# Softmax over rows of 512: two loads queued when group 8 has been scaled, and a store directly behind them

## The chip, the cores and the metric

The kernel runs on one core of a Trainium2 chip. The metric is the device time of one execution in microseconds (us), the median of several runs. The engines that matter are VectorE (DVE), ScalarE (ACT), GpSimd (POOL) and SyncE (SP). SyncE computes nothing here: it waits on semaphores and issues the DMA transfers, all of them into one queue that is served by 16 DMA engines.

## The reference

```python
x = np.random.randn(16, 1024, 512).astype(np.float32)

def reference(x):
    x_max = np.max(x, axis=-1, keepdims=True)
    exp_x = np.exp(x - x_max)
    return (exp_x / np.sum(exp_x, axis=-1, keepdims=True)).astype(np.float32)
```

It is a softmax over the last axis: 16,384 rows of 512 numbers. The input is 33.55 MB and the output as much.

## The kernel before

The rows are dealt to the 128 partitions, so each partition has 128 rows. Eight rows of every partition are a group, and there are 16 groups. Two groups, 16 rows or 4 MB, are a block; every transfer moves one block, so there are 8 loads and 8 stores. In this document load n and store n are those of block n, which holds groups 2n and 2n+1.

The data stays in one buffer in SBUF, `held`, in which all is computed in place. It is a ring of 12 groups (`RING`), six blocks. Loads 0 to 5 therefore fill it, and load 6 goes to the place of block 0, load 7 to that of block 1, once stores 0 and 1 have landed.

For each group, VectorE takes the row maxima with the sign changed (`rowmax`, line 169). ScalarE takes the exponential of each row with that as its bias and sums it (line 213). VectorE takes the reciprocal of the sums (line 177). Then the group is multiplied by it (`scale`, line 183), on GpSimd for groups 0 to 11 and on VectorE for groups 12 to 15. The string `VECTOR` gives VectorE's order by hand: M for maxima, P for a reciprocal whose product GpSimd makes, V for one whose product VectorE makes. The end of a group's product raises the semaphore `scaled[g]`.

SyncE's order is written out in `ORDER`: loads 0 to 5 (`AHEAD` of them without a wait), stores 0 to 2, loads 6 and 7, stores 3 to 7. SyncE runs through this list strictly in order; a wait holds up everything behind it. The loop of lines 144 to 158 puts the waits in:

- Ahead of a load it waits for the store that frees the place (line 148).
- Ahead of a store it waits for `scaled` of the store's two groups, and for one more group where `AFTER` names one (line 153). Each group is waited for once, at the first place that asks for it (`done`).

`AFTER` is `{(0, 16): 4, (48, 64): 11, (80, 96): 12}`: store 0 also waits for group 4, store 3 for group 11 and store 5 for group 12. The helper `take` (line 114) is a wait on a semaphore that sets it back.

Of the kernel before, what the change touches and what calls it, by code (L numbers as in the profile page):

```python
# [14 lines left out]
GROUPS = 16  # L15
# [25 lines left out]

AFTER = {(0, 16): 4, (48, 64): 11, (80, 96): 12}

# [29 lines left out]
def kernel(  # L77
# [5 lines left out]
    nc = tc.nc  # L83
# [7 lines left out]
    def in_dram(rows, a, b):  # L91

        first, last = next(k for k in BLOCKS if k[0] <= a and b <= k[1])
        block = rows[first * P : last * P].rearrange("(p r) d -> p r d", p=P)
        return block[:, a - first : b - first, :]
# [9 lines left out]
    scaled = [nc.alloc_semaphore(f"scaled{g}") for g in range(GROUPS)]  # L105
# [6 lines left out]
    def take(engine, semaphore, n):  # L112

        engine.wait_ge(semaphore, n).then_inc(semaphore, -n)  # L114

    def rows(a, b):
        assert a // RING == (b - 1) // RING
        return held[:, a % RING : (b - 1) % RING + 1, :]

    def meets(k, a, b):  # L120
        return k[0] < b and a < k[1]

    def group(g):
        return g * GROUP, (g + 1) * GROUP
# [4 lines left out]
    def load(k):  # L129
        copy = nc.sync.dma_start(out=rows(*k), in_=in_dram(x_rows, *k))  # L130
        copy.then_inc(loaded[k], 16)
        return copy
# [9 lines left out]

    taken, done = set(), set()
    for what, k in ORDER[AHEAD:]:
        if what == "L":
            for s in stores:
                if meets(s, k[0] - RING, k[1] - RING) and s not in taken:
                    take(nc.sync, stored[s], 16)
                    taken.add(s)
            load(k)  # L150
        else:
            for g in range(GROUPS):
                if (meets(k, *group(g)) or AFTER.get(k) == g) and g not in done:
                    take(nc.sync, scaled[g], 1)
                    done.add(g)
            nc.sync.dma_start(out=in_dram(out_rows, *k), in_=rows(*k)).then_inc(
                stored[k], 16
            )
# [34 lines left out]
    for step in VECTOR.split():  # L193
        what, g = step[0], int(step[1:])
# [62 lines left out]
```

## Time and profile before

| what | value |
|---|---|
| median of 3 runs | 159.81 us (159.57 to 159.94) |
| profiled execution | 160.33 us, of which its span from first to last instruction 159.0 us |
| VectorE, ScalarE, GpSimd busy | 90.0, 92.0, 83.9 us |
| DMA | 2304 packets, 67.11 MB, 422 GB/s over the span |
| load, issue to landing | median 30.3 us of 8, 4096 KB each |
| store, issue to landing | median 21.6 us of 8, 4096 KB each |

A load or store is issued by SyncE and then stands in the queue; issue to landing holds the time in the queue too. SyncE's instructions are not counted as busy. A transfer's issue is called by line 130 if it is a load and by line 156 if it is a store. The profiled execution lies 0.52 us above the median of the runs, and 1.33 us of it lie outside the span.

### The profile page before, as it was taken

What the parts mean: (1) busy time and instruction counts of PE and PEld (TensorE: products, weight loads), DVE (VectorE), ACT (ScalarE), POOL (GpSimd) and SP (SyncE); (2) the same over time, 40 slices, a digit from 0 to 9 for tenths busy, and PEclk for the clock granted to TensorE, in tenths of its full rate; (3) what the DMA queues carried; (4) which work ended last, traced back from release to release, by engine and by line L of the source; (5) the groups of instructions that cost most, each with busy time, mean ns of one, the idle gap of its engine ahead of it and who ended that gap; (6) DMA issues with size and microseconds to landing.
All of it is one profiled execution on the core that took longest, in us unless ns stands there. A gap on an engine that the chain in (4) does not pass through costs nothing. (4 is left out here: it accounts for less than half of the span.)

```text
span 159.0 us, 720 instructions
## 1 busy us (share of the span) xinstructions
DVE 90.0 (57%) x36; ACT 92.0 (58%) x257; POOL 83.9 (53%) x16
## 2 busy tenths in 40 slices
DVE  0008959777977977887700000695999996920000
ACT  0300699999999999999993000049946749000000
POOL 0000009999999999999999999990000000000000
DMA  7999999999999999999999999999999999999994
GB/s 264 453 462 404 404 503 412 396 453 462 404 396 511 412 396 437 478 404 396 503 412 404 387 396 495 429 396 445 478 396 396 495 429 396 429 486 404 396 495 173
DMA packets 2304, 67.11 MB, mean 422 GB/s; under 512 B 256, under 2 KB 256, under 8 KB 256
## 3 DMA queue, kind: packets, MB, share of 16 engines
q1 hardware_dynamic: 2304, 67.11, 98.5%
HBM read 33.55 MB, written 33.55 MB: 422 GB/s over the span
## 5 line engine op out<-in xcount | busy, mean ns | idle before, releaser
L213 ACT ACTIVATE held<-held,shift x128 | 90.3, 709 | 39.3 <-ACTq L114 39.3
L183 POOL TENSOR_TENSOR held<-held,recip 128x4096 f32<-128x4096 f32 x12 | 83.7, 7012 | 23.1 <-POOLq L114 23.1
L169 DVE TENSOR_REDUCE shift<-held 128x8 f32<-128x4096 f32 x16 | 70.3, 4401 | 27.9 <-DVEq L114 27.9
L213 ACT ACTIVATION_READ_ACCUMULATOR held<-held,shift x128 | 24.2, 189 | 0.0
L183 DVE TENSOR_TENSOR held<-held,recip 128x4096 f32<-128x4096 f32 x4 | 17.7, 4425 | 0.1
L177 DVE RECIPROCAL recip<-sums 128x8 f32<-128x8 f32 x16 | 3.2, 202 | 21.9 <-ACT held L213 19.9
L206 ACT ACT_TABLE_LOAD x1 | 1.3, 1283 | 4.0 <-PEq L141 4.0
L241 POOL MEMSET const-float32-0.0<- 128x1 f32 x1 | 0.1, 98 | 0.2 <-issue 0.2
L241 POOL MEMSET const-bfloat16-1.0<- 128x1 bf16 x1 | 0.1, 101 | 0.0
L241 POOL MEMSET const-uint8-127<- 128x1 uint8 x1 | 0.1, 101 | 0.0
L241 POOL MEMSET const-float32-1.0<- 128x1 f32 x1 | 0.1, 98 | 0.0
## 6 DMA issues: line engine op xcount, KB each, us to landing
held<-in_x_dram SPq DMA_DIRECT2D x8, 4096.0 KB, 30.3
out_dram<-held SPq DMA_DIRECT2D x8, 4096.0 KB, 21.6
```

Of the source, the lines that this page charges most:

```text
L169: nc.vector.reduce_max(out=stats(shift, g), in_=rows(*group(g)), axis=AX, negate=True).then_inc(maxed, 1)
L177: ratio = nc.vector.reciprocal(out=stats(recip, g), in_=stats(sums, g))
L183: product = engine.tensor_mul(out=rows(*group(g)), in0=rows(*group(g)), in1=stats(recip, g).unsqueeze(2).to_broadcast([P, GROUP, d]),)
L206: nc.scalar.preload_act_table(EXP)
L213: act = nc.scalar.activation(out=row, in_=row, func=EXP, bias=shift[:, at], scale=1.0, accum_out=sums[:, at],)
L241: nc = _bacc.Bacc("TRN2", target_bir_lowering=False, num_devices=1)
```

## The change

`AFTER` now names loads as well as stores, by the kind and the first row. The loop that waits for groups has moved ahead of the distinction between load and store, so it also runs for a load. Load 6 waits for group 8. Store 3 no longer waits for group 11, but only for its own groups 6 and 7. Store 0 still waits for group 4 and store 5 for group 12. The order of the transfers in `ORDER` is the same.

```diff
-AFTER = {(0, 16): 4, (48, 64): 11, (80, 96): 12}
+AFTER = {("S", 0): 4, ("L", 96): 8, ("S", 80): 12}
...
     for what, k in ORDER[AHEAD:]:
+        for g in range(GROUPS):
+            due = AFTER.get((what, k[0])) == g or (what == "S" and meets(k, *group(g)))
+            if due and g not in done:
+                take(nc.sync, scaled[g], 1)
+                done.add(g)
         if what == "L":
             for s in stores:
                 if meets(s, k[0] - RING, k[1] - RING) and s not in taken:
...
             load(k)
         else:
-            for g in range(GROUPS):
-                if (meets(k, *group(g)) or AFTER.get(k) == g) and g not in done:
-                    take(nc.sync, scaled[g], 1)
-                    done.add(g)
             nc.sync.dma_start(out=in_dram(out_rows, *k), in_=rows(*k)).then_inc(
                 stored[k], 16
             )
```

The waits of SyncE, in its order, from load 6 on:

| transfer | before waits for | after waits for |
|---|---|---|
| load 6 | store 0 | group 8, store 0 |
| load 7 | store 1 | store 1 |
| store 3 | groups 6, 7, 11 | groups 6, 7 |
| store 4 | groups 8, 9 | group 9 |
| store 5 | groups 10, 12 | groups 10, 11, 12 |
| store 6 | group 13 | group 13 |
| store 7 | groups 14, 15 | groups 14, 15 |

## The prediction

> **What bounds the kernel now.** I read the page first, because it says which resource is full.
>
> ```profile
> span 159.0 us, 720 instructions
> DVE 90.0 (57%) x36; ACT 92.0 (58%) x257; POOL 83.9 (53%) x16
> DMA  7999999999999999999999999999999999999994
> q1 hardware_dynamic: 2304, 67.11, 98.5%
> ```
>
> No compute engine is busy for more than 58% of the span. The one DMA queue is busy for 98.5% of it, full in every slice but the first and the last. So the kernel ends when the sixteenth transfer of 4 MB has passed through this queue, and a compute engine matters only if it lets the queue run dry. The page's chain that ended last (DVE 3%, ACT 3%) only leads to the issue of the last store and doesn't carry the span.
>
> Next I asked for single transfers: the issue by SyncE (first and last start are the same for one transfer) and its time to landing. These are, in order, load 0, store 0, load 6 and store 3.
>
> ```profile
> L130 SPq DMA_DIRECT2D held<-in_x_dram x1: 383/383/383, 0.0 to 0.0; - x1
> DMA to landing us min/median/max: 12.3/12.3/12.3
> L156 SPq DMA_DIRECT2D out_dram<-held x1: 348/348/348, 58.6 to 58.6; - x1
> DMA to landing us min/median/max: 12.0/12.0/12.0
> L130 SPq DMA_DIRECT2D held<-in_x_dram x1: 340/340/340, 70.6 to 70.6; - x1
> DMA to landing us min/median/max: 30.0/30.0/30.0
> L156 SPq DMA_DIRECT2D out_dram<-held x1: 343/343/343, 107.4 to 107.4; - x1
> DMA to landing us min/median/max: 12.9/12.9/12.9
> ```
>
> Issue plus time to landing, with the issue from the timeline to 0.01 us, gives for all sixteen: loads 0 to 5 land at 12.3, 22.0, 31.7, 41.4, 51.1 and 60.8; stores 0 to 2 at 70.6, 80.3 and 90.1; loads 6 and 7 at 100.6 and 110.5; stores 3 to 7 at 120.3, 129.9, 139.7, 149.3 and 159.0. They land strictly in the order of issue, 9.7 us apart, except that load 6 takes 10.5 behind store 2, and load 7 takes 9.9. So 12.3 + 15 x 9.7 = 157.8, plus 1.0 at loads 6 and 7, plus 0.2 of rounding and small excesses: 159.0. The turn from stores to loads is the only place where the queue loses anything between its ends. The landing events of the sixteen DMA engines show how: of store 2 the last part lands 0.08 us behind the fifteenth, of load 6 it lands 0.71 us behind (100.61 against 99.90), and it stays the last to the end (158.97).
>
> Last I looked at what would release the loads in the new order, group 8 on GpSimd:
>
> ```profile
> 79.36 7.01 POOL L183 TENSOR_TENSOR held<-held,recip 128x4096 f32<-128x4096 f32 x1
> 86.33 7.01 POOL L183 TENSOR_TENSOR held<-held,recip 128x4096 f32<-128x4096 f32 x1
> ```
>
> GpSimd scales groups 0 to 11 back to back from 23.56 us, so the first row is group 8. It ends at 86.37, and the second row is group 9, done at 93.34.
>
> **The change part by part.** The order of the sixteen transfers stays as it is, and so do the bytes. Only issue times move.
>
> *Load 6 waits for group 8.* It was issued at 70.64, as soon as store 0 had landed. SyncE needs 0.10 us from the end of group 4 (58.47) to the issue of store 0 (58.57), and 0.09 from group 11 (107.29) to store 3 (107.38), so load 6 now goes at 86.37 + 0.09 = 86.46, that is 15.8 us later. Store 0's landing is long past by then. Is that late for the queue? Store 2 is issued at 65.54, ahead of the new wait, and holds the queue until 90.1. The rows above give what a transfer needs from issue to landing with little or nothing before it: 12.3 for a load into an empty queue, 12.0 and 12.9 for stores issued 2.2 and 3.1 us before the transfer ahead landed. Load 6 would need 86.46 + 12.3 = 98.8, while its turn gives 100.6, or 90.1 + 9.7 = 99.8 if the queue lost nothing at the turn. The cover is 1.8 us, and still 1.0 us in the better case. Cost: zero, hidden by store 2. If the cover is gone, each further microsecond is paid in full at the end, as the queue has no slack later on.
>
> *Behind that wait on SyncE* stand load 7, store 3 and store 4. Load 7 went at 80.38. Two issues with two waits between them stand 0.53 apart (58.57 and 59.10), so load 7 goes by about 87.0, 13 us ahead of its turn. Zero. VectorE waits for loads 6 and 7 before the row maxima of groups 12 and 14; these land as before, so it starts at 100.75 as now.
>
> *Store 3 directly behind load 7.* Groups 6 and 7 end at 72.42 and 79.39, so it goes by about 87.5 and not at 107.38. Its turn comes when load 7 lands at 110.5, and the present issue was 3.1 us ahead of that with a step of 9.8: there is 0.1 us to be had here at most. Zero. Store 4 now waits for group 9, so it goes at 93.34 + 0.1 = 93.4 and not at 107.91, and lands when its turn comes. Store 5 waits for group 12 as before (issued at 116.06, its turn at 129.9), so from there on nothing moves. Store 7, issued at 140.08, is 9.2 us ahead of store 6's landing, against the 2.2 that sufficed for store 0.
>
> *The turn at load 6* is the one term whose price after the change no row shows. Its loss is 1.0 us with the load queued 19 us ahead. Queued 3.7 us ahead, it lies between a gain of 1.0 (no loss left) and a loss: the empty queue's start-up, 12.3 - 9.7 = 2.6 us, paid in full after store 2 in place of the 1.0, which is 1.6 more. I take no change, since the nearest row, store 0 issued 2.2 us ahead of its turn, lost nothing by the short notice, and load 0's 12.3 fits under store 2 with 1.8 to spare.
>
> *Sum:* 0 + 0 + 0. The profiled execution took 160.33, 1.33 more than its span, and 0.52 more than the median of the runs. I forecast no change to either, so 159.81 us, written as 159.8. A measurement of this kernel can tell about 0.2%, 0.3 us, from no change.
>
> **The rivals.** *The load comes late (slower).* This is the one place where the change can lose: load 6 stands in the queue 3.7 us before store 2 lands. It decides if a load needs more than 100.6 - 86.5 = 14.1 us from issue to landing behind a running store. For it: no row has a load issued so late behind a store, and load 0 ran with no stores beside it. Against it: 12.0, 12.3 and 12.9 are all below 14.1. If the whole start-up of 2.6 us comes in place of the 1.0, that is 1.6 more: 161.4. If half of the 1.6 shows, which I hold for the middle of this case: 160.6. The Trainium skill, "DMA: Bandwidth & Descriptors", section "Rules for kernel authors", speaks for this rival: it says to issue a DMA early, so that its fixed set-up cost is overlapped. By that rule holding back a load can only cost. The trace agrees in part only: store 0, held until 2.2 us ahead of its turn, lost nothing, and load 6, queued 19 us ahead, is the one that lost.
>
> *The turn gets cheaper (faster).* The single late engine costs 0.7 us and the turn 1.0 in all. If the delay comes from loads and stores standing in the rings together, engines that finish their share early start on load 6 while others still write, and a load held back has less of that. For it: the loss sits exactly there, and the two turns where the next transfer was queued late (stores 0 and 3, 2.2 and 3.1 us ahead) lost at most 0.1. Against it: both of those turns are from loads to stores; a load's first packets may have to wait for their data whenever they are queued, as the 2.6 us of load 0 suggest. If the late engine falls into line: 159.81 - 0.7 = 159.1. If all is gone: 158.8. The section "Latency and other measured facts" of the same page gives HBM access latency as 0.2 us on average and 2 us at high load; that would lie at the turn whenever the load is queued, and by it this rival has no gain.
>
> *Early stores cost.* Stores 3 and 4 now stand behind the loads for 20 us. If that gave the turn from load 7 to store 3 the 0.7 us of the late engine, the time would be 160.5. Nothing in the trace speaks for it, except that the loads which waited long are the ones that lost.
>
> **How the numbers follow.** No change 0.38; the turn cheaper 0.35, since the loss is real, its cause is unknown and the change touches just that place; load late 0.20 and early stores 0.07, together 0.27 for slower. The range runs from 159.0, nearly the whole gain, to 160.7, just over the middle price of a late load; outside lie the full gain and the full start-up, 2 in 10 together. The likeliest case's own range is 159.5 to 160.1.
>
> **What would show it.** Right: load 6 issued at 86.5, load 7 and store 3 within 1.1 us behind, store 4 at 93.4; load 6 still lands at 100.6 and store 2 at 90.1; the queue stays at 98.5%. Load late: the step from store 2 to load 6 is over 10.5 us and everything behind moves by as much. Turn cheaper: that step is below 10.2, and the last engine's part lands close behind the fifteenth. Early stores: the step of store 3 grows from 9.8 to some 10.5. I am wrong altogether if store 2's landing moves, as nothing ahead of it is touched.

## The result and the profile after

The changed kernel takes 160.31 us (median of 5 runs, 160.17 to 160.65) against 159.74 before (5 runs, 159.57 to 159.94). The ratio is 1.0039, with a 95% interval of 1.0022 to 1.0056. So it is slower by 0.57 us, where no change was forecast. The time lies inside the stated range of 159.0 to 160.7, near the 160.5 of the third rival, early stores, which had a chance of 0.07.

The page of the kernel after, first the lines that answer to those of before:

```profile
span 159.1 us, 720 instructions
DVE 90.1 (57%) x36; ACT 92.0 (58%) x257; POOL 83.9 (53%) x16
DMA  7999999999999999999999999999999999999996
q1 hardware_dynamic: 2304, 67.11, 98.9%
```

Nothing here tells what happened. The queue is even a little busier than before (98.9% against 98.5%), since a packet that takes longer counts as busy for longer. And the span is only 0.1 us above the 159.0 of the profiled execution of before. That one was a slow example of its kernel: in the runs beside the experiments the spans of the kernel before have a median of 158.3 to 158.4, while the five of the kernel after are 158.8 to 159.3, median 159.0. The difference to be explained is therefore 0.6 to 0.7 us of span, of which two single profiles show 0.1.

Group 8 on GpSimd, and then load 6, load 7 and store 3, each with its issue and its time to landing:

```profile
79.19 7.02 POOL L185 TENSOR_TENSOR held<-held,recip 128x4096 f32<-128x4096 f32 x1
```

```profile
L131 SPq DMA_DIRECT2D held<-in_x_dram x1: 339/339/339, 86.4 to 86.4; - x1
DMA to landing us min/median/max: 13.6/13.6/13.6
L131 SPq DMA_DIRECT2D held<-in_x_dram x1: 1107/1107/1107, 86.8 to 86.8; - x1
DMA to landing us min/median/max: 23.8/23.8/23.8
L158 SPq DMA_DIRECT2D out_dram<-held x1: 347/347/347, 88.1 to 88.1; - x1
DMA to landing us min/median/max: 32.3/32.3/32.3
```

Load 6 goes at 86.37 us and lands at 99.93, 9.9 behind store 2 (90.00) in place of 10.5: the hold cost nothing. Load 7 lands at 110.67, a step of 10.7 in place of 9.9. Store 3 lands at 120.40, 9.7 behind it. So the time is lost just before load 7 lands, at the turn from loads to stores.

The packets show it best. Every packet of 32 KB normally takes 1.213 us on its DMA engine, so I cut the trace into stretches of 1.21 us. The last two numbers of a row are the DMA share and the GB/s. At 433 GB/s exactly 16 packets, one for each engine, started in the stretch, and the share then says how many packet times they took. These are the stretches with the last packets of load 7, in the kernel before and in the kernel after:

```profile
106.10:107.31 1.21, 1.21 (x1) 1.21 (x5) 1.19 (x1) 1.00 1.00 433
107.31:108.52 1.21, 1.21 (x1) 1.21 (x5) 0.00 (x0) 1.00 1.00 433
```

```profile
106.10:107.31 1.21, 1.21 (x1) 1.21 (x5) 1.03 (x1) 1.00 1.09 433
107.31:108.52 1.21, 1.21 (x1) 1.21 (x5) 0.00 (x0) 1.00 1.57 433
```

Before, the packets took their normal time up to the turn. After, sixteen packets took 1.57 times as long, on average 0.57 x 1.21 = 0.69 us more, with another 0.1 us in the row above. Added up packet by packet (duration less 1.213 us, over all packets near the turn, divided by 16), the turn at store 3 loses 0.80 us per engine after and 0.02 before. The turn at load 6 loses 0.42 after and 0.53 before, the turn at store 0 0.02 in both. I call this sum the loss of a turn from here on. The balance is 0.78 - 0.11 = 0.7 us.

Each loss is taken from one profiled execution. All kernels of this document start alike, and their first packets lose between 0.6 and 0.8 us, in one of them 1.1. So a difference of 0.2 us between two losses says little.

### The profile page after: what moved, and what is told of

Read it like the earlier page. It is cut to its first block, busy times and chain, and to the rows that moved or that the text cites. A ratio compares the mean times of both kernels' runs of the same rounds, so it can differ in the third digit from the quotient of the medians.

```text
span 159.1 us, 720 instructions
## 1 busy us (share of the span) xinstructions
DVE 90.1 (57%) x36; ACT 92.0 (58%) x257; POOL 83.9 (53%) x16
## 3 DMA queue, kind: packets, MB, share of 16 engines
q1 hardware_dynamic: 2304, 67.11, 98.9%
```

## The experiments

In all of them the holds are written as in the changed kernel, and a line `+AFTER` stands in the place of its `AFTER`; the kernel before would be `{("S", 0): 4, ("S", 48): 11, ("S", 80): 12}`. The lead of a transfer is the time from its issue to the landing of the one ahead of it. The leads of before are 2.2 us (store 0), 19 us (load 6) and 3.1 us (store 3).

**Both held.** Load 6 as in the changed kernel, store 3 as before:

```diff
-AFTER = {("S", 0): 4, ("L", 96): 8, ("S", 80): 12}
+AFTER = {("S", 0): 4, ("L", 96): 8, ("S", 48): 11, ("S", 80): 12}
```

> Load 6 held for group 8, and store 3 held for group 11 as in the kernel before. Theory A (a store queued some 20 us ahead of its turn behind a load costs 0.8 us at that turn; holding the load costs nothing): the turn at store 3 loses under 0.1 us, the time is that of the kernel before or up to 0.3 us less, 159.4 to 159.8. Rival B (the loss comes from load 6, load 7 and store 3 being issued in one burst; load 7's issue took 1.11 us in it in place of 0.34): loads 6 and 7 are still issued 0.5 us apart, so part of the loss stays, about 160.0. Rival C (holding load 6 is what costs, and the loss shows at the next turn): 160.3 as the changed kernel.

159.53 us against 159.68, ratio 0.9984 (0.9973 to 0.9995). The stretch of load 7's last packets:

```profile
107.31:108.52 1.21, 1.21 (x1) 1.21 (x5) 0.51 (x1) 1.00 1.00 433
```

No loss at store 3, though load 7's issue took its 1.11 us here too:

```profile
L131 SPq DMA_DIRECT2D held<-in_x_dram x1: 1107/1107/1107, 87.5 to 87.5; - x1
```

So the hold of load 6 (rival C) is not the cause, and two loads issued in a burst cost nothing at this turn. A burst with store 3 in it is what remains of rival B. This version is faster than both kernels, by 0.16% against the one before. The losses of its profile don't show why: the turn at load 6 lost 0.66 us, and the three turns 0.70 against 0.57 before.

**Store 3 early, loads not held:**

```diff
+AFTER = {("S", 0): 4, ("S", 80): 12}
```

> Loads 6 and 7 are not held (issued at 70.6 and 80.4 us, as before); store 3 goes directly behind load 7, at 80.9. Theory A: the turn at store 3 loses 0.8 us, time 160.3 to 160.6, the changed kernel's or slightly more. Rival B: load 6 is 10 us ahead of the other two and load 7's issue takes 0.34, so no loss: 159.7 as before. Rival C: no loss: 159.7.

160.36 against 159.68, ratio 1.0048 (1.0031 to 1.0066). Load 7's last two packet times:

```profile
106.10:107.31 1.21, 1.21 (x1) 1.21 (x5) 1.02 (x1) 1.00 1.28 433
107.31:108.52 1.21, 1.21 (x1) 1.21 (x5) 0.00 (x0) 1.00 1.45 433
```

The two rows alone give 0.73 x 1.21 = 0.88 us; the loss at the turn is 0.87. The early store costs the whole difference by itself, with the loads queued as in the kernel before.

**Store 3 held for group 10**, issued at 100.25 us with load 7 already running:

```diff
+AFTER = {("S", 0): 4, ("S", 48): 10, ("S", 80): 12}
```

> As the kernel before, but store 3 is held for group 10 and not 11: issued at 100.4 us, when load 7 has just begun and 10 us ahead of its turn in place of 3. Theory A has no figure for where early begins: if the loss grows with the time in the queue in proportion (0.8 for 22 us), 0.3 us, so 160.0; if a store must only not stand there while another load is ahead of the running one, none: 159.7; if anything over the 3 us of before is early, 0.8: 160.5. Rivals B and C: 159.7.

160.49 against 159.68, ratio 1.0047 (1.0033 to 1.0061). The last packets of load 7:

```profile
106.10:107.31 1.21, 1.21 (x1) 1.21 (x5) 1.03 (x1) 1.00 1.30 433
107.31:108.52 1.21, 1.21 (x1) 1.21 (x5) 0.00 (x0) 1.00 1.22 379
```

At 379 GB/s fourteen packets started in the second row, and they took 1.22 where 14/16 = 0.88 would be normal. The loss at the turn is 0.81. A lead of 11 us (111.58 less 100.25) costs as much as one of 23 or 30, so the loss doesn't grow with the time in the queue. Load 7 was issued 20 us ahead of store 3 here (at 80.15), so there is no burst, and rival B is out too. (The profiled execution, 161.39 us, is the slowest of its six.)

**Store 0 early**, issued at 37.7 us, 23 us ahead of its turn:

```diff
+AFTER = {("S", 48): 11, ("S", 80): 12}
```

> As the kernel before, but store 0 is not held for group 4: issued at 37.6 us, 23 us ahead of its turn behind load 5. The other holds are as before. Theory A, if it is about any turn from load to store: the turn at store 0 loses 0.8 us, time 160.5. Rivals B and C: no burst there and no held load, so 159.7.

160.18 against 159.68, ratio 1.0030 (1.0018 to 1.0042). Two stretches with the last packets of load 5, and one at the turn from store 2 to load 6:

```profile
57.21:58.42 1.21, 1.21 (x1) 1.21 (x5) 1.21 (x1) 1.00 1.32 433
58.42:59.63 1.21, 1.21 (x1) 1.21 (x5) 1.21 (x2) 1.00 1.23 406
...
87.51:88.72 1.21, 0.00 (x0) 0.00 (x0) 1.21 (x1) 1.00 1.00 433
```

In the kernel before the same stretches read:

```profile
57.21:58.42 1.21, 1.21 (x1) 1.21 (x5) 1.21 (x1) 1.00 1.01 433
58.42:59.63 1.21, 1.21 (x1) 1.21 (x5) 1.21 (x2) 1.00 1.01 433
...
87.51:88.72 1.21, 0.00 (x0) 0.00 (x0) 1.21 (x1) 1.00 1.32 433
```

The turn at store 0 loses 0.75 us, as theory A had it. But the turn at load 6, which loses 0.53 before, loses 0.01 here. That was not expected, and it agrees with a time 0.3 us below the expected 160.5.

**Both stores early:**

```diff
+AFTER = {("S", 80): 12}
```

> Neither store 0 nor store 3 is held, nor are the loads; so store 0 is issued at 37.7 us and store 3 at 80.9. The runs so far show 0.75 to 0.87 us lost at a turn from load to store with the store early, and 0.4 to 0.6 at the turn from store 2 to load 6, except that with store 0 early alone the turn at load 6 lost 0.01. Theory A1 (each early store pays its own turn, and an early turn to stores also takes away the loss at the next turn to loads): losses 0.75 + 0 + 0.8 against 0.5 before, so 1.0 more: 160.7. Theory A2 (the 0.01 was chance): 1.5 more, 161.2. Theory A3 (what is lost once by an early store is not lost again): as with store 0 early alone, 160.2.

160.12 against 159.67, ratio 1.0028 (1.0018 to 1.0037). Losses: 0.81 at store 0, 0.00 at load 6, 0.01 at store 3. The last packets of load 7:

```profile
107.31:108.52 1.21, 1.21 (x1) 1.21 (x4) 0.00 (x0) 1.00 1.01 433
```

So A3, the last of the three, is the one that fits. The same early store 3 that costs 0.8 us in the changed kernel costs nothing when store 0 was early too.

**How early is early?** Store 0 held until group 6's exponentials were done (lead 4.1 us), and until half of them were done (lead 7.1 us). The holds of the other transfers are those of the kernel before:

```diff
+        if (what, k[0]) == ("S", 0):
+            nc.sync.wait_ge(expd, 6)     # second kernel: wait_ge(half, 7)
...
+            if r == 3:                   # second kernel, in ScalarE's loop
+                act.then_inc(half, 1)
```

> As the kernel before, but store 0 is held until the exponentials of group 6 are done (56.8 us): 4.0 us ahead of load 5's landing in place of 2.2. If the loss begins only when the store is queued before the engines work on the last 4 or so microseconds of the load ahead: none, 159.7. If any lead over 3 us costs: 0.75, time 160.2 to 160.5.

159.63 against 159.67, ratio 0.9996 (0.9987 to 1.0006). Losses: 0.32 at store 0, 0.15 at load 6, none at store 3. Their sum, 0.47, is near the 0.57 of the kernel before, in another place, and the time is the same.

> As the kernel before, but store 0 is held until half of group 6's exponentials are done (about 54.0 us): 6.8 us ahead of load 5's landing; a semaphore of ScalarE is added for it. A lead of 10 us cost the whole 0.8 and one of 3.1 nothing. A threshold below 6.8: 0.75 lost, 160.2 to 160.5. A threshold above: 159.7. A gradual loss: between.

160.11, ratio 1.0030 (1.0020 to 1.0039), the time of a store 0 queued 23 us ahead. Losses: 0.42 at store 0 and none behind it. The profiled execution also lost 1.11 us at its first packets, against 0.6 to 0.8 elsewhere, so its loss at store 0 may not be typical; the time, a median of ten runs, is. By the times, then, the price sets in between leads of 4.1 us (none) and 7.1 us (that of 23); by the packets, part of it is there at 4.1 already.

**Store 0 early, load 6 and store 3 held:**

```diff
+AFTER = {("L", 96): 8, ("S", 48): 11, ("S", 80): 12}
```

> Store 0 early (37.7 us), load 6 held for group 8, store 3 held for group 11. If an early turn to stores takes away the loss at the next turn to loads whenever the loads are queued: as with store 0 early alone, 160.2. If it needs the loads queued early too: the turn at load 6 loses 0.4 to 0.6 again, 160.6.

160.09 against 159.67, ratio 1.0021 (1.0010 to 1.0032). Losses 0.76, 0.01 and 0.02: what the early store does to the next turn doesn't depend on when the loads are queued.

**Five turns in place of three.** From these runs came theory D: the first store that is queued early behind a load costs about 0.8 us, and no later turn costs anything. To tell it from a price for each turn, load 6 went between stores 1 and 2:

```diff
-    ("S", (32, 48)),
     ("L", (96, 112)),
+    ("S", (32, 48)),
     ("L", (112, 128)),
```

With store 0 early:

> Load 6 goes between stores 1 and 2, so the queue turns five times and not three: store 1 to load 6, load 6 to store 2, store 2 to load 7 and load 7 to store 3 follow load 5 to store 0. Store 0 is early (37.7 us), store 3 held for group 11. Theory D (two states: the first early store behind a load costs the engines 0.75 us once, and after that no turn costs anything): 160.1, as with three turns. Theory P (each turn is paid by itself: some 0.8 for a store queued early, 0.4 to 0.6 for a load): 0.75 + 0.5 + 0.8 + 0.5 against 0.5 before, 161.7.

160.16 against 159.66, ratio 1.0030 (1.0005 to 1.0056). Losses: 0.83 at store 0, then at most 0.03 at each of four turns. Theory P's 161.7 is far off. In the four kernels with store 0 early by 23 us the losses add up to 0.78 to 0.90 against 0.57 before. That is 0.2 to 0.3 us of the 0.4 to 0.5 by which they are slower; where the rest lies isn't shown.

With store 0 held:

> The same five turns, with store 0 held for group 4 as in the kernel before; store 2 then stands 19 us early behind load 6. Theory D: 0 at store 0, 0.5 at load 6, 0.8 at store 2 (the one early store), 0 at load 7 and at store 3, 1.3 in all against 0.5: 160.4. Theory P: 0.5 + 0.8 + 0.5, 1.8 in all: 160.9.

160.64 against 159.66, ratio 1.0051 (1.0030 to 1.0073). The last packets of load 6, ahead of the early store 2, and then the stretches around the turn from store 2 to load 7:

```profile
86.90:88.11 1.21, 0.00 (x0) 0.00 (x0) 1.21 (x1) 1.00 1.25 433
88.11:89.32 1.21, 0.00 (x0) 0.00 (x0) 1.21 (x1) 1.00 1.46 433
...
97.00:98.21 1.21, 1.21 (x1) 1.21 (x5) 1.21 (x1) 1.00 1.00 433
98.21:99.42 1.21, 1.21 (x1) 1.21 (x5) 1.21 (x1) 1.00 1.00 433
99.42:100.63 1.21, 0.95 (x1) 1.21 (x4) 1.21 (x2) 1.00 1.01 433
```

Losses: 0.02 at store 0, 0.69 at load 6, 0.86 at store 2, then 0.00 at load 7 and at store 3. That is theory D's sequence; the sum of 1.57 is 1.0 above the 0.57 of the kernel before, and the times differ by 0.98. Both prices are larger than the expected 0.5 and 0.8, so the time alone lies between the two theories; the turn at load 7, which loses nothing, tells them apart. This run settles one more point. In the other kernels with an early store the next store came early with it (in the changed kernel store 4, at 93.28 us and not 107.91). Here store 2 is the only early one, so one is enough.

**Load 6 held longer.** For a lead of 2 us, with store 3 held for group 11 and load 6 not for group 8, VectorE reads five rows of group 11 again and SyncE waits for that:

```diff
+        if g == 11:
+            idle = nc.vector.reduce_max(
+                out=scrap[:, 0:5], in_=rows(88, 93), axis=AX, negate=True
+            )
+            idle.wait_op(expd, 11, "sem-ge")
+            idle.then_inc(late, 1)
...
+        if (what, k[0]) == ("L", 96):
+            take(nc.sync, late, 1)
```

> Stores 0 and 3 held for groups 4 and 11; load 6 held until VectorE has read five rows of group 11 once more (a maximum that nobody uses, some 2.8 us from 85 us on), so it is issued at about 87.9, 2.2 us ahead of store 2's landing in place of 3.4. If a load held until 2 us before its turn turns as freely as stores do at that lead: the 0.5 at load 6 is gone, 159.2. If the loss at load 6 does not hang on the lead (0.51 at 19 us, 0.66 at 3.4): 159.5 to 159.7. If it comes late by the prediction's measure (87.9 + 12.3 = 100.2 against a turn of 99.8): 0.4 lost, no more than now, 159.6.

160.34 against 159.66, ratio 1.0040 (1.0021 to 1.0059). About 0.25 us of it lie outside the span (160.30 with a span of 158.7, where the other kernels have 1.3 between the two). Load 6 was issued a little later than planned, at 88.31, 1.8 us ahead of store 2's landing, and its engines' parts land at a median of 20.2 us behind those of store 1, where it is 19.8 in the kernel before:

```profile
88.31 0.34 SPq L133 DMA_DIRECT2D held<-in_x_dram  x1
```

```profile
DMA to landing us min/median/max: 12.3/12.3/12.3
```

A load can't be held to 2 us as a store can: its landing is now its issue plus 12.3, and the span is some 0.4 us longer (median 158.7 against 158.3). Added up from the packet records, the 16 engines stood idle for 0.3 us each around this turn, and for none in the kernel with both held. Their packets lost 0.68 here and 0.66 there.

And held for group 9 in place of 8:

```diff
+AFTER = {("S", 0): 4, ("L", 96): 9, ("S", 48): 11, ("S", 80): 12}
```

> Stores 0 and 3 held for groups 4 and 11, load 6 held for group 9 in place of group 8, so issued at about 93.4. By the prediction's measure it lands 12.3 us after that, at 105.7 in place of 100.4, so 5.3 us are lost: 164.8. If store 3, which is now some 8 us ahead of its turn, is early by that: 165.5. If the queue makes the lost time good (some slack behind it): below 164.

166.57 against 159.66, ratio 1.041 (1.036 to 1.046). Load 6, issued at 93.73, when the queue had been empty since store 2 landed at 90.08, again takes 12.3 us and lands at 106.06, 5.5 behind its landing of before. Store 3 is now 9.4 us ahead of its turn, and load 7's last packets show it:

```profile
112.30:113.51 1.21, 1.21 (x1) 1.21 (x5) 0.00 (x0) 1.00 1.14 433
113.51:114.72 1.21, 1.21 (x1) 1.21 (x5) 0.00 (x0) 1.00 1.83 433
```

The loss there is 1.18, so 5.5 + 1.2 = 6.7 of the 6.9 us; the expected 165.5 had too little for both terms. Store 3 is early here only because the load is late, and load 7's packets pay for it all the same.

## Why the prediction was wrong

*The step that failed* is the term for store 3: "there is 0.1 us to be had here at most. Zero." Its price was 0.80 us. I priced it by the present issue, 3.1 us ahead of its turn, as if a longer lead could only be safer. But the change takes the lead from 3.1 to 22.6 us (110.67 less 88.12), and both turns from load to store that the trace showed had leads of 2.2 and 3.1. No row showed an early store. The term should have been bounded from both sides, as I did for load 6, with the 1.0 us of the one turn whose transfer had waited long as the nearest price.

*The rival that came true* is "Early stores cost", at 160.5 with a chance of 0.07. That its price of 0.7 was close to the 0.80 measured is luck: the 0.7 was the lag of one late engine behind load 6, while the 0.80 is lost by the packets of all 16 engines. It is luck too that the range held the result, as its upper end was the price of a late load. The rival's sentence that only the transfers that waited long had lost was the right hint, given too little weight. The place was one transfer off: I looked for the loss in the step of store 3 (9.8 to 10.5), but it is in the step of load 7 (9.9 to 10.7), since the last packets of the load are the ones stretched.

*Load 6's hold: zero, and right.* It was issued at 86.37 (86.46 forecast), landed at its turn, and with store 3 left as it was the time is 159.53 against 159.68. The measure behind it, issue plus 12.3 us, held to 0.1 us in the two kernels where the load did come late (12.3 in both). The late-load rival asked for more than 14.1 us, and 12.3 was enough behind a running store too (issued 1.8 us ahead). The rule of the Trainium skill that spoke for that rival ("DMA: Bandwidth & Descriptors", "Rules for kernel authors", issue a DMA early) is borne out for the load only when its lead falls from 3.3 us (no cost) to 1.8 us (some 0.4 us of span); for the store the measurement goes the other way, as issuing it early is what costs.

*The cheaper turn* (0.35) didn't come from the hold: the turn at load 6 loses 0.37 to 0.69 with leads of 3.3 to 20 us alike, where no early store came before it. That it can be free at all (0.00 to 0.01 after an early store 0) was not foreseen. The late engine on which I built that rival, 0.7 us behind the others to the end, is not in every execution: in the kernel with both held the last part of load 6 lands 0.12 us behind the fifteenth. By the packets this turn lost 0.53 us before, and not the 1.0 that I read from the landings. The sign that I gave for this rival did appear in the profile after (a step of 9.9 us, the last two parts 0.10 apart), but the kernel with both held shows it too (10.0 and 0.12) while its packets lose 0.66 at that turn. So the sign tells that no engine is late, and not that the turn is cheaper. The 0.7 were not there to be gained in most runs, as the median of 159.7 beside the profiled 160.33 already said.

*Load 7, store 4 and what follows*: load 7 at 86.83 and store 4 at 93.28, as forecast (87.0 and 93.4). Load 7's issue took 1.11 us in place of 0.34 and put store 3 at 88.12 and not 87.5; in the first experiment load 7's issue took as long, and nothing was lost at store 3. VectorE was released by load 6 at 100.06 us and the tail had its slack, as forecast.

*What stays open* is the mechanism. The runs show that the first store queued 9 us or more ahead behind a load stretches that load's last packets by 0.75 to 0.87 us per engine, 1.18 in one case, and that no later turn in the same execution costs anything. They don't show what the engines hold differently from then on, nor why the turn to a load, free in that case, costs about 0.5 otherwise.

## What to carry to other kernels

Where one DMA queue is full from end to end, the issue time of a transfer can still matter, although its place in the queue doesn't change: here a store queued 2 to 3 us ahead of its turn behind a load was free, and one queued 7 to 30 us ahead cost 0.4 to 1.2 us of each engine's time, mostly 0.8, the first time. Price a transfer that is moved from late to early as an unknown of either sign, not as zero. When a single profile of each version differs by less than the medians do, look at the packets of each turn, and not at the span or at the queue's busy share, which rises when packets get slower.

## What the runs showed of the hardware that was not expected

- After one early store the turns between loads and stores are free to the end: four turns lost at most 0.03 us each after a first one of 0.83.
- A load issued 1.8 us before a running store landed took 12.3 us from issue to landing (88.31 to 100.58), and so did one issued 3.7 us after the queue had run empty (93.73 to 106.06). Load 0, at the start, takes 12.1 to 12.8 in the profiles.
- An issue by SyncE took 1.1 us in place of 0.34 in several kernels with three or more transfers in the queue (load 7 in the kernel after and in the one with both held, store 3 in the one with store 3 early alone). In the one with both held no cost of it shows. Load 7 of the kernel before took 0.34 with as many, so the number alone doesn't decide it.
